# Split weight tiles moved by 64 bytes where they are TensorE's stationary operand

## The chip, the cores and the metric

The kernel runs on one core of one Trainium2 chip. The time is the device time of one execution in microseconds (us). Before the change it is 2506.83 us, the median of 3 runs (2505.83 to 2507.53).

## The reference

Three layers follow each other on one sequence of 256 tokens of width 2048, all in float32: a block of sliding-window attention and a gated feed-forward, a recurrent mLSTM layer, and a band-attention layer with modulated inputs. Cut to its matrix products:

```python
h = rms_norm(x, mixer_norm)
x = x + attention(h @ w_qkv) @ w_o                                    # first block
x = x + (silu(h2 @ w_gate) * (h2 @ w_up)) @ w_down                    # width 5632
y = mlstm(modulated(x) @ a_w_in) @ a_w_out                            # second block, layer 1
x = x + gate_0 * rmsnorm(y, g_post_0)
k, v = modulated(x) @ kv_w;  q, z = modulated(x) @ b_w_in             # second block, layer 2
y = (band_attention(q, k, v) * silu(z)) @ b_w_out
x = x + gate_1 * rmsnorm(y, g_post_1)
```

With it come products of one vector `c` with `ada_w` and `kv_ada_w`, which give the shifts, scales and gates.

## The kernel before

All weights are streamed once from memory in tiles `w` of 128 partitions x 2 k-tiles x 512 columns (512 KB, 4096 bytes in each partition). Float32 accuracy is bought with three fast products in the format fp32r: ScalarE rounds a weight tile to `wh`, VectorE takes the rest `wl = w - wh`, and the activations have been split in the same way into `xh`, `xl` (or `ah`, `al`). TensorE then adds high x high, high x low and low x high (function `products`, line 267).

There are two ways round. In a chunk of mode "tok" the activations are stationary (128 tokens are loaded as weights of the array) and 512 columns of `wh` or `wl` are streamed through it. In a chunk of mode "wst" 128 columns of `wh` or `wl` are loaded, so they are the stationary operand, and the 256 tokens of `xh` or `xl` are streamed. Mode "wst" is used where the result is wanted with features on the partitions: for q and k of the mLSTM layer (8 chunks, one for each head, each followed by three of mode "tok"), for k of the band attention (4 chunks) and for its q and z (8 chunks). Each of these 20 chunks has 16 k-tiles x 4 column blocks x 3 products = 192 matmuls. A trace names a matmul by its output and then the streamed and the stationary operand: `mm<-wh,xh` is mode "tok", `mm<-xh,wh` is mode "wst".

The list `order` has all slots (a weight tile of a chunk) one after the other. `stream_load` (line 138) issues the DMA of a slot from SyncE up to 4 slots ahead, into 3 buffers; `stream_split` (line 146) splits a slot up to 3 ahead, into 4 buffers of `wh` and 4 of `wl`, which are used in turn whatever the mode. Work beside it (softmax, norms, transposes, the vector products) is fed in between by a planner that counts times of its own (`pump`, `stall`); TensorE's part in it has outputs named `bg`.

The memory of a partition is given out in the order of the pools: `keep` first, with `cols`, `onesr`, `mods`, `x`, `xh`, `xl`, `ah`, `al`, `big`; then `strm` with the 3 buffers of `w`, 4 of `wh`, 4 of `wl` and 2 of `mvt`; then `rest`, `small`, and the pool of the phase (`p1` to `p4`). The buffers of one name lie one behind the other at the tile's size. In the last phase this reaches almost to the end of the memory, with `sq` of pool `p4` as its last tile: a scratch tile of 2048 bytes a partition into which `fin_half` (line 1235) has ScalarE write squares that nobody reads (only their sum is kept).

Of the kernel before, what the change touches and what calls it, by code (L numbers as in the profile page):

```python
# [10 lines left out]
F32 = mybir.dt.float32  # L11
F32R = mybir.dt.float32r
# [6 lines left out]
P = 128  # L19
# [2 lines left out]
KD = D // P  # L22
SL = 2
CW = 512
NEG = -1.0e30
EPS = 1e-6
DFF = 5632
# [53 lines left out]
def kernel(ctx: ExitStack, tc: tile.TileContext, i: dict, out: bass.AP):  # L81
# [6 lines left out]
    strm = ctx.enter_context(tc.tile_pool(name="strm", bufs=1))  # L88
    rest = ctx.enter_context(tc.tile_pool(name="rest", bufs=1))
    small = ctx.enter_context(tc.tile_pool(name="small", bufs=4))  # L90
    psp = ctx.enter_context(tc.tile_pool(name="psp", bufs=8, space=PSUM))

    live = [0, 0]
    mmres = [4]
    ver = {"x": [0] * KD, "a": [0] * KD}
# [21 lines left out]
    xh = keep.tile([P, KD, T], F32R, name="xh")  # L117
# [15 lines left out]
    order = []  # L133
# [4 lines left out]
    def stream_load(upto):  # L138
        while cnt["load"] < min(upto, len(order)):
            ch, s = order[cnt["load"]]  # L140
            w = strm.tile([P, SL, CW], F32, tag="w", bufs=3, name="w")
            ch.load(s, w)
# [3 lines left out]
    def stream_split(upto):  # L146
        while cnt["split"] < min(upto, len(order)):
            j = cnt["split"]
            w = loaded.pop(j)
            clk.cur = 0.0  # L150
            wh = strm.tile([P, SL, CW], F32R, tag="wh", bufs=4, name="wh")
            S.copy(wh, w)
            wl = strm.tile([P, SL, CW], F32R, tag="wl", bufs=4, name="wl")
            V.tensor_sub(wl, w, wh.bitcast(F32))
            split[j] = (wh, wl, clk.cur)
            cnt["split"] += 1
# [54 lines left out]
    def wload(w, r0, c0):  # L211
        def f(s, t):
            a = w[r0 + s * SL * P:r0 + (s + 1) * SL * P, c0:c0 + CW]
            nc.sync.dma_start(out=t, in_=a.rearrange("(k p) n -> p k n", p=P))
# [11 lines left out]
    def do_group(idxs):  # L226
        staged = len(idxs) > 1
        ch, s0 = order[idxs[0]]
        for k in range(s0 * SL, (s0 + len(idxs)) * SL):
            while ver[ch.need[0]][k] < ch.need[1][k]:  # L230
                stall()
        stream_load(idxs[0] + 1 + PF)
        stream_split(idxs[0] + 1 + SP)
        if s0 == 0:
            shp = [P, CW] if ch.mode == "tok" else [P, 2, T]
            while live[0] + live[1] > 6:
# [3 lines left out]
        for ts in ((0,), (1,)) if staged else ((0, 1),):  # L240
            for j, idx in enumerate(idxs):
                s = order[idx][1]
                if j and ts[0]:
                    stream_load(idx + 1 + PF)
                    stream_split(idx + SP)
                wh, wl, t_w = split.pop(idx) if ts[-1] else split[idx]
                for k in range(SL):
                    kt = s * SL + k
                    clk.cur = max(t_w, rdy[ch.need[0]][kt])
                    products(ch, kt, k, wh, wl, ts)  # L250
                    ch.k = kt + ts[-1]
                    if not staged:
                        mv_step()
                    if kt < ch.nk - 1:
                        pump()
            if s == ch.ns - 1:
                clk.cur = clk.eng["pe"]
                if ch.part is not None:
                    for t in ts:
                        ch.part(ch.ps, t)  # L260
                if ts[-1]:
                    if not (ch.done and ch.done(ch.ps)):
                        mm_free()
                    ch.ps = None
                pump()
# [52 lines left out]
    def mv_jobs():  # L318
        for lab, w, c0, b, kind, dst in (
                [("A", i["ada0"], j * CW, i["ada_b"][0:1, j * CW:(j + 1) * CW], "col", (0, j // 4, j % 4))  # L320
                 for j in range(8)]
# [134 lines left out]
        return b.rearrange("p a b -> p (a b)")  # L456

    def sumsq(junk_pool, src, dst, scale=1.0):
        j = junk_pool.tile([P, CW], F32, tag="sq", bufs=1, name="sq")
        S.activation(j, src, ACTF.Square, scale=scale, accum_out=dst)  # L460

    def xt_pair(m):
# [83 lines left out]
    ssx = rest.tile([P, 2, 4], F32, name="ssx")  # L546
# [208 lines left out]
    def resid(n, ps, pool, after):  # L755
        for t in range(2):
            c = x[:, t, n * CW:(n + 1) * CW]
            V.tensor_add(c, ps[t], c)
            sumsq(pool, c, ssx[:, t, n:n + 1])
        add_bg(after(n))  # L760
# [36 lines left out]
    pools = {}  # L797
# [50 lines left out]
    def down_part(ps, t):  # L848
        c = x[:, t, 3 * CW:]
        V.tensor_add(c, ps[t], c)  # L850
        sumsq(pools["q2"], c, ssx[:, t, 3:4])
        if t:
            add_bg(xt_raw(3, raw))
# [146 lines left out]
    def num_task(h, v):  # L1000
# [22 lines left out]
        for t in range(2):  # L1023
            sumsq(q3, nm[t], ss[:, t:t + 1], scale=rd[:, t:t + 1])
# [143 lines left out]
    def band_head(g, j):  # L1168
# [5 lines left out]
        nc.sync.dma_start(out=bi, in_=bass.AP(tensor=rel.tensor, offset=h * 383, ap=[[1, P], [1, T]]))  # L1174
        G.memset(bi[0:64, 0:64], NEG)
        yield 1
# [57 lines left out]

    def fin_half(ps, t, n):
        c = pools["yy"][:, t, n * CW:(n + 1) * CW]
        sumsq(pools["q4"], ps[t], ssx[:, t, n:n + 1])
        V.tensor_mul(c, ps[t], gt[1][:, n * CW:(n + 1) * CW])

    def fin_done(n):  # L1240
        def f(ps):
            for t in range(2):
                fin_half(ps, t, n)
        return f

    def fin_part(ps, t):
        fin_half(ps, t, 3)
        x_rstd((t,))
        for n in range(4):
            c = x[:, t, n * CW:(n + 1) * CW]  # L1250
            y = pools["yy"][:, t, n * CW:(n + 1) * CW]
            if n == 3:
                S.activation(y, y, ACTF.Copy, scale=rst[:, t:t + 1])
                G.tensor_add(c, c, y)
            else:
                V.scalar_tensor_tensor(c, y, rst[:, t:t + 1], c, op0=ALU.mult, op1=ALU.add)
        for n in range(4):
            nc.sync.dma_start(out=out[t * P:(t + 1) * P, n * CW:(n + 1) * CW], in_=x[:, t, n * CW:(n + 1) * CW])
# [39 lines left out]
    S.activation(warm, ones[:, 0:1], ACTF.Exp)  # L1298
    stream_load(1)
    stream_split(1)  # L1300
    load_x(0)
    nc.sync.dma_start(out=cols, in_=i["cols"])
# [35 lines left out]
def _lay(inputs):  # L1338
# [10 lines left out]
    r = np.arange(P)  # L1349
    lo = np.where(r[None, :] <= r[:, None], f(0), f(NEG)).astype(f)  # L1350
    up = np.where(r[None, :] > r[:, None], f(0), f(NEG)).astype(f)
    ge = np.where(r[None, :] >= r[:, None], f(0), f(NEG)).astype(f)
    inv = np.power(10000.0, -np.arange(0, 64, 2) / 64.0).astype(f)
# [33 lines left out]
```

## Time and profile before

| | |
|---|---|
| median of 3 runs | 2506.83 us (2505.83 to 2507.53) |
| the profiled execution | 2509.79 us, of which its span 2508.0 us |
| TensorE, matmuls | 97% of the span |
| VectorE, ScalarE, GpSimd | 70%, 48%, 7% |
| mean granted TensorE clock | 0.989 of full |
| read from memory | 571.25 MB, 229 GB/s over the span |

The span runs from the first to the last instruction. Matmuls overlap in the pipeline, so the duration of one is longer than the time between two starts; what a stream of matmuls costs is read from the starts.

### The profile page before, as it was taken

To read this page: it belongs to the slowest core of one execution; us is meant where nothing else is said; L and a number is where in the kernel's file an instruction comes from. 1 tells how busy PE (TensorE), PEld (TensorE's weight loads), DVE (VectorE), ACT (ScalarE), POOL (GpSimd) and SP (SyncE) were. 2 spreads that over 40 slices of the span, in tenths; PEclk is the share of its full clock that TensorE was granted. 3 is DMA by queue.
4 is the path that set the end of the run, shared out by engine and by line. 5 is a ranking of instruction groups with operands and counts; after the bars stand their busy time and mean duration, and the time that the engine had idled before them with its cause. 6 is when DMAs were issued, how large, how long until landed. Compare 5 with 4: busy or idle time off the path is not lost.

```text
span 2508.0 us, 34570 instructions
## 1 busy us (share of the span) xinstructions
PE 2438.4 (97%) x12782; PEld 2076.4 (83%) x12782; DVE 1752.8 (70%) x2577; ACT 1210.1 (48%) x1654; POOL 173.4 (7%) x174
## 2 busy tenths in 40 slices
PE   8989999999999999899999999999999899999998
PEld 6867888887888888778888788888888789899986
DVE  6885777777777777768778777755454664577765
ACT  5665544334443444554445444445444544555553
POOL 0232000000000000201101100101101120000000
PEclk9989999999999999999999999999999999999999
DMA  6524788888888887568878788856556456678854
GB/s 211 157 96 143 238 285 284 286 275 279 287 283 291 285 286 267 159 213 269 264 250 273 267 286 277 261 170 192 182 169 196 151 151 186 193 254 263 259 188 153
DMA packets 319226, 575.63 MB, mean 230 GB/s; under 512 B 21680, under 2 KB 56752, under 8 KB 319056
## 3 DMA queue, kind: packets, MB, share of 16 engines
q1 hardware_dynamic: 319056, 573.42, 70.8%
q8 instruction: 100, 1.64, 0.3%
q14 instruction: 70, 0.57, 0.1%
HBM read 571.25 MB, written 2.10 MB: 229 GB/s over the span
## 4 chain that ended last, share of the span: by engine, by line
PE 77%; DVE 7%; DMA 6%; issue 4%; ACT 4%; POOL 2%; SPq 0%; ACTq 0%; DVEq 0%; POOLq 0%
PE mm L66 72%; PE bg L66 5%; DVE wl L66 3%; ACT wh L66 2%; DMA w<-in_a_w_in_dram 2%; DVE mvacc L66 2%; DMA w<-in_w_gate_dram 1%; DMA w<-in_w_down_dram 1%; POOL big L66 1%; DMA w<-in_w_qkv_dram 1%; ACT big L66 1%; POOL y L66 0%; DMA w<-in_a_w_out_dram 0%; POOL so L66 0%; ACT sq L66 0%
## 5 line engine op out<-in xcount | busy, mean ns | idle before, releaser
L66 DVE TENSOR_TENSOR wl<-w,wh 128x1024 fp32r<-128x1024 f32 x816 | 1009.3, 1244 | 620.9 <-ACT wh L66 605.4
L66 ACT CAST wh<-w 128x1024 fp32r<-128x1024 f32 x816 | 854.9, 1051 | 957.1 <-PE mm L66 598.8
L66 PE MATMUL mm<-wh,xh 128*128 128x512 f32 x1760 | 691.4, 393 | 0.0
L66 PE MATMUL mm<-wh,xl 128*128 128x512 f32 x1760 | 686.8, 390 | 3.8 <-DVE xl L66 3.8
L66 PE MATMUL mm<-wl,xh 128*128 128x512 f32 x1760 | 686.8, 390 | 3.0 <-DVE wl L66 3.0
L66 DVE SCALAR_TENSOR_TENSOR mvacc<-mvt,sc,mvacc 128x512 f32<-128x512 f32 x512 | 392.2, 766 | 10.1 <-issue 0.5
L66 PEld LDWEIGHTS mm<-wh,xl 128*128 128x128 f32 x1760 | 331.1, 188 | 74.3 <-DVE xl L66 4.7
L66 PEld LDWEIGHTS mm<-wl,xh 128*128 128x128 f32 x1760 | 331.2, 188 | 72.2 <-DVE wl L66 5.1
L66 PEld LDWEIGHTS mm<-wh,xh 128*128 128x128 f32 x1760 | 331.2, 188 | 70.5 <-issue 2.6
L66 PE MATMUL mm<-xh,wh 128*128 128x256 f32 x1280 | 370.0, 289 | 7.9 <-DVE xh L66 7.9
L66 PE MATMUL mm<-xl,wh 128*128 128x256 f32 x1280 | 367.5, 287 | 1.0 <-DVE xl L66 0.9
L66 PE MATMUL mm<-xh,wl 128*128 128x256 f32 x1280 | 365.6, 286 | 0.0
L66 PE MATMUL mm<-wh,al 128*128 128x512 f32 x864 | 337.8, 391 | 3.5 <-DVE al L66 3.5
L66 PE MATMUL mm<-wh,ah 128*128 128x512 f32 x864 | 340.3, 394 | 0.0
L66 PE MATMUL mm<-wl,ah 128*128 128x512 f32 x864 | 337.5, 391 | 0.0
L66 PEld LDWEIGHTS mm<-xh,wh 128*128 128x128 f32 x1280 | 249.2, 195 | 11.6 <-DVE xh L66 5.5
L66 PEld LDWEIGHTS mm<-xl,wh 128*128 128x128 f32 x1280 | 249.1, 195 | 4.4 <-DVE xl L66 3.5
L66 PEld LDWEIGHTS mm<-xh,wl 128*128 128x128 f32 x1280 | 249.1, 195 | 0.0
L66 PEld LDWEIGHTS mm<-wh,al 128*128 128x128 f32 x864 | 163.0, 189 | 38.1 <-DVE al L66 3.9
L66 PEld LDWEIGHTS mm<-wh,ah 128*128 128x128 f32 x864 | 162.9, 189 | 36.7 <-issue 3.3
L66 PEld LDWEIGHTS mm<-wl,ah 128*128 128x128 f32 x864 | 163.0, 189 | 33.2 <-DVE wl L66 0.3
L66 POOL TENSOR_TENSOR so<-so,sz 128x512 f32<-128x512 f32 x16 | 29.6, 1851 | 711.8 <-DVE mvacc L66 361.8
(191 smaller groups left out, 1303.2 us busy)
## 6 DMA issues: line engine op xcount, KB each, us to landing
mvt<-in_ada_dram SPq DMA_DIRECT2D x192, 512.0 KB
w<-in_a_w_in_dram SPq DMA_DIRECT2D x192, 512.0 KB
w<-in_w_gate_dram SPq DMA_DIRECT2D x88, 512.0 KB
w<-in_w_up_dram SPq DMA_DIRECT2D x88, 512.0 KB
w<-in_w_down_dram SPq DMA_DIRECT2D x88, 512.0 KB
mvt<-in_kv_ada_dram SPq DMA_DIRECT2D x64, 512.0 KB
w<-in_a_w_in_dram SPq DMA_DIRECT2D x128, 256.0 KB
w<-in_a_w_out_dram SPq DMA_DIRECT2D x64, 512.0 KB
```

The costliest lines, as they stand in the source:

```text
L66: return fn(*a, **k)
```

## The change

`wh` and `wl` are now taken from tiles that are 16 elements (64 bytes) longer. For a slot of mode "wst" the tile's data begin 64 bytes behind the start of the tile, for one of mode "tok" at its start. The eight tiles need 512 bytes more in each partition; in the last phase the scratch tile `sq` is given up for it, and the squares go into the first two k-tiles of `xh`.

```diff
+ROOM = 16
...
+    def offset_tile(tag, off):
+        t = strm.tile([P, SL * CW + ROOM], F32R, tag=tag, bufs=4, name=tag)
+        return t[:, off:off + SL * CW].rearrange("p (k n) -> p k n", n=CW)
...
             w = loaded.pop(j)
+            off = ROOM if order[j][0].mode == "wst" else 0
             clk.cur = 0.0
-            wh = strm.tile([P, SL, CW], F32R, tag="wh", bufs=4, name="wh")
+            wh = offset_tile("wh", off)
             S.copy(wh, w)
-            wl = strm.tile([P, SL, CW], F32R, tag="wl", bufs=4, name="wl")
+            wl = offset_tile("wl", off)
             V.tensor_sub(wl, w, wh.bitcast(F32))
...
     def sumsq(junk_pool, src, dst, scale=1.0):
-        j = junk_pool.tile([P, CW], F32, tag="sq", bufs=1, name="sq")
+        if junk_pool is None:
+            j = xh[:, 0:2].rearrange("p k t -> p (k t)")
+        else:
+            j = junk_pool.tile([P, CW], F32, tag="sq", bufs=1, name="sq")
         S.activation(j, src, ACTF.Square, scale=scale, accum_out=dst)
...
-        sumsq(pools["q4"], ps[t], ssx[:, t, n:n + 1])
+        sumsq(None, ps[t], ssx[:, t, n:n + 1])
```

## Rows read from the trace of the kernel before

**Rows 1.** The page's busy times by engine, its line of granted clock in 40 slices, and the chain of work that ended last, by engine and by line.

```profile
PE 2438.4 (97%) x12782; PEld 2076.4 (83%) x12782; DVE 1752.8 (70%) x2577; ACT 1210.1 (48%) x1654; POOL 173.4 (7%) x174
...
PEclk9989999999999999999999999999999999999999
...
PE 77%; DVE 7%; DMA 6%; issue 4%; ACT 4%; POOL 2%; SPq 0%; ACTq 0%; DVEq 0%; POOLq 0%
PE mm L66 72%; PE bg L66 5%; DVE wl L66 3%; ACT wh L66 2%; DMA w<-in_a_w_in_dram 2%; DVE mvacc L66 2%; DMA w<-in_w_gate_dram 1%; DMA w<-in_w_down_dram 1%; POOL big L66 1%; DMA w<-in_w_qkv_dram 1%; ACT big L66 1%; POOL y L66 0%; DMA w<-in_a_w_out_dram 0%; POOL so L66 0%; ACT sq L66 0%
```

**Rows 2.** The page's costliest groups of instructions: busy us, mean ns of one, then idle time before them. The two splits, and one of the three matmul forms of each kind (the other two forms of a kind have the same count).

```profile
L66 DVE TENSOR_TENSOR wl<-w,wh 128x1024 fp32r<-128x1024 f32 x816 | 1009.3, 1244 | 620.9 <-ACT wh L66 605.4
L66 ACT CAST wh<-w 128x1024 fp32r<-128x1024 f32 x816 | 854.9, 1051 | 957.1 <-PE mm L66 598.8
L66 PE MATMUL mm<-wh,xh 128*128 128x512 f32 x1760 | 691.4, 393 | 0.0
...
L66 PE MATMUL mm<-xh,wh 128*128 128x256 f32 x1280 | 370.0, 289 | 7.9 <-DVE xh L66 7.9
...
L66 PE MATMUL mm<-wh,ah 128*128 128x512 f32 x864 | 340.3, 394 | 0.0
```

**Rows 3.** Timeline of TensorE in the chunks 2 to 4 of the band attention's k (mode "wst"): start us, duration us. The first two and the last two of 576 matmuls.

```profile
2039.92 0.28 PE L66 MATMUL mm<-xh,wh 128*128 128x256 f32 x1
2040.04 0.28 PE L66 MATMUL mm<-xl,wh 128*128 128x256 f32 x1
...
2108.80 0.28 PE L66 MATMUL mm<-xl,wh 128*128 128x256 f32 x1
2108.92 0.28 PE L66 MATMUL mm<-xh,wl 128*128 128x256 f32 x1
```

**Rows 4.** Timeline of TensorE in the feed-forward (mode "tok"). The first and the last of 25 matmuls in a row.

```profile
410.72 0.39 PE L66 MATMUL mm<-wh,xl 128*128 128x512 f32 x1
...
416.16 0.39 PE L66 MATMUL mm<-wh,xl 128*128 128x512 f32 x1
```

**Rows 5.** Timeline of TensorE in the first chunk of the mLSTM layer (mode "wst"), at half clock (see rows 6). The first and the last of 11 matmuls in a row.

```profile
1024.91 0.41 PE L66 MATMUL mm<-xh,wl 128*128 128x256 f32 x1
...
1027.04 0.41 PE L66 MATMUL mm<-xh,wh 128*128 128x256 f32 x1
```

**Rows 6.** Table by stretch: us, busy us of PE, PEld, DVE, ACT and POOL with instructions begun or running, granted clock, busy share of the DMA engines, GB/s. The stretch of rows 5; the first chunk of the band attention's k; its chunks 2 to 4; its eight chunks of q and z.

```profile
1024.50:1027.00 2.50, 2.50 (x13) 2.50 (x13) 1.89 (x3) 2.50 (x4) 2.50 (x4) 0.50 0.00 0
...
2007.00:2040.00 33.00, 29.32 (x193) 26.39 (x194) 27.31 (x42) 18.30 (x27) 13.58 (x15) 0.90 0.37 113
...
2040.00:2109.00 69.00, 69.00 (x577) 69.00 (x576) 29.41 (x24) 28.23 (x30) 0.00 (x0) 1.00 0.64 191
...
2196.00:2409.00 213.00, 212.25 (x1752) 210.49 (x1751) 162.28 (x303) 116.61 (x190) 3.58 (x18) 1.00 0.77 251
```

**Rows 7.** Timeline of TensorE in the gates of the mLSTM layer: fp32r matmuls with 40 stationary columns at a pitch of 160 bytes for each k-tile. The first, two in the midst, and the last of 48, and the matmul after them.

```profile
1060.97 0.28 PE L66 MATMUL bg<-xh,wgh 128*40 128x256 f32 x1
...
1061.55 0.28 PE L66 MATMUL bg<-xh,wgl 128*40 128x256 f32 x1
1061.66 0.28 PE L66 MATMUL bg<-xh,wgh 128*40 128x256 f32 x1
...
1066.46 0.28 PE L66 MATMUL bg<-xh,wgl 128*40 128x256 f32 x1
1066.58 0.40 PE L66 MATMUL mm<-wh,xh 128*128 128x512 f32 x1
```

**Rows 8.** Timeline of TensorE around one of the pairs that sum up a gate vector over the partitions (`mv_reduce`), inside a chunk of mode "wst".

```profile
2344.77 0.28 PE L66 MATMUL mm<-xh,wl 128*128 128x256 f32 x1
2344.89 0.28 PE L66 MATMUL bg<-acch,onesr 128*128 128x256 f32 x1
2345.00 0.28 PE L66 MATMUL bg<-accl,onesr 128*128 128x256 f32 x1
2345.12 0.28 PE L66 MATMUL mm<-xh,wh 128*128 128x256 f32 x1
```

**Rows 9.** Timeline of TensorE behind two interruptions by other matmuls: in mode "wst", 8 matmuls from the second one on (first and last shown), then in mode "tok", 6 matmuls from the second one on (first and last shown).

```profile
2224.11 0.28 PE L66 MATMUL mm<-xl,wh 128*128 128x256 f32 x1
...
2224.93 0.28 PE L66 MATMUL mm<-xh,wl 128*128 128x256 f32 x1
...
417.50 0.39 PE L66 MATMUL mm<-wl,xh 128*128 128x512 f32 x1
...
418.66 0.39 PE L66 MATMUL mm<-wh,xh 128*128 128x512 f32 x1
```

**Rows 10.** The tile `sq`: its instructions in the last stage, duration ns min/median/max, first and last start us; and the last matmul of mode "wst" in the timeline.

```profile
L66 ACT ACTIVATE sq<-mm x8: 597/598/599, 2447.8 to 2497.8; 128x512 f32<-128x512 f32 x8
...
2408.33 0.28 PE L66 MATMUL mm<-xh,wl 128*128 128x256 f32 x1
```

**Rows 11.** Who waited for whom between 2040 and 2409 us: us in total, times, longest us.

```profile
DVE wl L66 <- ACT wh L66: 112.8, 83, 3.7
ACT wh L66 <- PE mm L66: 97.6, 66, 2.1
ACT wh L66 <- DMA w<-in_b_w_in_dram: 26.8, 17, 3.6
```

## The prediction

> **What bounds the kernel now.** I read the page first: TensorE is busy for 97% of the span at full clock but for a few moments, and matmuls are 77% of the chain that ended last [rows 1]. So what counts is the time from one matmul's start to the next, and I went on to the timeline. In mode "wst" 576 matmuls start from 2039.92 to 2108.92 us without a break: 69.00 us over 575 steps is 120.0 ns each [rows 3]. In mode "tok" 24 steps take 5.44 us, 226.7 ns each [rows 4]. The groups give the counts: 3 x 1280 = 3840 matmuls of mode "wst" and 3 x (1760 + 864) = 7872 of mode "tok" [rows 2]. At these steps they are 461 and 1784 us, together 90% of the span.
>
> What would a step be without any loss? A chunk of mode "wst" that begins at half clock shows it: 10 steps take 2.13 us, 213 ns [rows 5], at a granted clock of 0.50, that is 1.2 GHz [rows 6]. This is 256 columns at one per cycle, with nothing on top (256 / 1.2 = 213.3). At full clock, 2.4 GHz, that would be 106.7 ns, so each step of 120.0 ns loses 13.3 ns. In mode "tok" 512 columns would be 213.3 ns, and the step of 226.7 loses the same 13.3 ns. The loss shows only where the streamed operand is read at full speed while the next stationary operand is loaded. That is what the change can aim at: two read streams of TensorE that get in each other's way because of where they begin.
>
> **The change part by part.** Nothing is added to or taken from the instructions: the same 816 splits, the same matmuls, the same DMAs and queues. What moves is addresses.
>
> *Where things lie before.* From `xh` to the first buffer of `wh` there are 5 x 16384 + 3 x 4096 = 94208 bytes, 23 x 4096, and every buffer is 4096 bytes long. The slices used are 512 or 1024 bytes apart. So both operands of every pair begin at the same place within any 512 bytes. The trace of the kernel before shows no other case in a long stream of 128 stationary columns.
>
> *Where they lie after.* A tile is now 4160 bytes long, and the four buffers lie behind each other: buffer n begins 64 x n bytes further within 256 bytes (`wl` likewise, since 4 x 4160 = 65 x 256). In mode "wst" the data then lie 64, 128, 192 and 256 bytes behind the activations' place, in mode "tok" 0, 64, 128 and 192. Within 128 bytes that is: every second slot of *both* modes is off by 64, not all of one and none of the other. The change does only half of what it says in mode "wst", and does in mode "tok" what it says it avoids.
>
> *Price of a shift in mode "wst".* Not in the trace, so from its nearest rows. Upper end of the gain: the whole loss, 13.3 ns. Lower end: none, or a loss, since a new offset can be worse. Between: in the gates, whose 40 stationary columns are at a new offset for each k-tile, 48 steps take 5.61 us, 116.9 ns each, and single steps go down to some 110 (the view rounds to 10 ns) [rows 7]. And the pair `acch`, `accl`, which by the allocation lies 64 bytes off `onesr` within 128, is entered from steps of 120 ns and takes 230 ns from 2344.89 to 2345.12, about 3 to 5 ns less a step [rows 8]. Against it: behind an interruption, where only the timing of the two streams has changed and no address, 7 steps take 0.82 us, 117 ns each [rows 9], before they settle at 120. So 117 needs no offset. Nearest row: a gain of 3 ns, which over half the matmuls is 3 x 1920 = 5.8 us. The first chunk of the band layer is paced by its activations (193 matmuls in 33 us, where 192 x 0.12 = 23 us [rows 6]), and the mLSTM's first one runs at half clock in part [rows 5], so 18 chunks of 20 count: 5.2 us at most from this row, and I take 0 for the forecast, because the same 117 is there without any shift.
>
> *Price of a shift in mode "tok".* Also unseen. Lower end: nothing, or a gain of up to 13.3 ns. On the other side stand the steps behind an interruption: 5 of them take 1.16 us, 232 ns each [rows 9], 5.3 ns more than the settled 226.7. So a change of phase between the two streams costs in this mode. Over half the matmuls, 3936, each ns is 3.9 us. Forecast 0; both ends go into the range.
>
> *The splits.* ScalarE (1051 ns) and VectorE (1244 ns) write the same bytes to other addresses [rows 2]. A slot of mode "wst" is 24 x 120 ns = 2.88 us, so both have more than half of it free in chunks 2 to 4 of k (29 and 28 us busy of 69 [rows 6]). Without that cover a 1% slower split would be 12 ns x 816 = 10 us; the cover is there. In the stretch of q and z VectorE is busy for 162 of 213 us [rows 6], and the split of `wl` waits 113 us in all for `wh`, mostly for buffers and data [rows 11]. A shorter step there would pass on less than whole.
>
> *The squares into `xh`.* Eight instructions of 598 ns, the first at 2447.8, write fp32r instead of f32, no wider. Their new wait, for the last matmul that reads `xh`, is met: it started at 2408.33 [rows 10], 39 us earlier. Nothing is queued behind a wait. Cost 0; without that cover it would be the end of that matmul, once.
>
> The sum: 2506.83 + 0. The profiled execution took 2509.79 us, 1.79 of them outside its span, and lies 0.12% above the median; differences of its rows are used against the median.
>
> A rule that speaks against the change: the Trainium skill, "SBUF — State Buffer", section "Who interferes with whom", gives TensorE two read ports, one for the streamed operand and one for the loads, independent, and says that it never waits on anyone. By that an offset changes nothing, and the sum is the forecast. The trace only half agrees: half clock has no loss, full clock loses 13.3 ns, which two free ports would not explain. The page "TensorE: Matmul & The Clock Gate", section "Wait — 56ns, not 53.3ns?", puts a fixed 2.5 ns on a matmul at full clock; by it the step could fall to 109.2 ns, an estimate of 10.8 x 3840 = 41 us for the whole of mode "wst". No run here shows such a step for 128 stationary columns.
>
> **The rivals.**
>
> *Faster: the offset frees the streams in mode "wst".* For it: the loss of 13.3 ns is there, and steps of fp32r between 110 and 120 ns are seen. Against: 40 stationary columns at many offsets still lose 10 ns. With 7 ns (half the loss) on half of 18 chunks, 1728 matmuls, it is 12 us: 2494.7. At the end of the bounds, 13.3 ns on half of them, 23 us: 2484; a gain of 3 ns in both modes (1728 and 3936 matmuls) would be 17 us: 2490.
>
> *Slower: the rotation of the buffers shifts the streamed tiles.* Every second slot of mode "tok" is off by 64 bytes. If that costs what a change of phase costs [rows 9], 5.3 x 3936 = 21 us are lost, and 3 x 1728 = 5.2 us won in the other mode: 2522.5. It decides from 1.3 ns a step on (5 us / 3936) where mode "wst" gains nothing, from 2.6 where it gains 3. For it: mode "tok" has twice the matmuls, and 232 ns is seen. Against: that row is a change of timing, not of address. If it held for three slots in four, 5904 matmuls, 31 less 8 us: 2530.
>
> *No change, since the change doesn't do what it says.* Either the loss belongs to the load itself and no address matters, or the shifts in both modes cancel. This is the forecast.
>
> **How the numbers follow.** Forecast, no difference: 0.40. Faster: 0.32. Slower: 0.28. About 0.2%, 5 us, is what a measurement of this kernel can tell from no change. The likeliest alone reaches from 2502 to 2511. The other two take the range to 2488 (about 0.1 lies below: most of the loss gone in the even slots) and 2525 (about 0.1 above: the streamed slots lose more than the row says).
>
> **What would show it.** Steps of 120 and 226.7 ns in all four buffers: no address matters, forecast right. Steps in mode "wst" that change from slot to slot (24 matmuls) with the buffer: an offset matters; their period, 2 or 4 slots, tells whether 128 or 256 bytes count. The same in mode "tok" decides the sign. I am wrong if the step of the shifted slots falls to near 107 ns, or if slots of mode "tok" pass 228 ns.

## The result, and the profile after

The changed kernel takes 2524.07 us (2521.41 to 2526.99, 4 runs) where the kernel before takes 2506.33 (2505.11 to 2507.53) beside it: a ratio of 1.0071, 95% interval 1.0054 to 1.0088, so 13.5 to 22 us slower. The time lies inside the range given (2488 to 2525), but the forecast, no difference, was wrong. Its profiled span is 2522.1 us.

First the page: busy times, the line of granted clock, the chain by engine, and three of the costliest groups (busy us, mean ns of one, idle time before).

```profile
PE 2456.7 (97%) x12782; PEld 2066.6 (82%) x12782; DVE 1757.8 (70%) x2577; ACT 1206.3 (48%) x1654; POOL 172.8 (7%) x174
...
PEclk9999999999999999999999999999999999999999
...
PE 78%; DVE 6%; DMA 5%; issue 5%; ACT 4%; POOL 2%; SPq 0%; ACTq 0%; DVEq 0%; POOLq 0%
...
L67 DVE TENSOR_TENSOR wl<-w,wh 128x1024 fp32r<-128x1024 f32 x816 | 1011.5, 1247 | 630.3 <-ACT wh L67 611.4
L67 ACT CAST wh<-w 128x1024 fp32r<-128x1024 f32 x816 | 852.3, 1048 | 972.3 <-PE mm L67 707.1
L67 PE MATMUL mm<-wh,xh 128*128 128x512 f32 x1760 | 697.6, 396 | 0.0
```

Against [rows 1, 2] only TensorE's matmuls have grown: 18.3 us more busy time with the same 12782 instructions at the same clock. The two splits cost what they did (1247 and 1048 ns), and the time that TensorE stands without a matmul has not grown (2522.1 less 2456.7 is 65.4 us, 69.6 before). So the time is again in the steps from one start to the next.

In mode "wst", the timeline of TensorE in chunk 2 of the band attention's k (start us, duration us). The first and the last matmul of each of four slots in a row.

```profile
2056.87 0.28 PE L67 MATMUL mm<-xh,wh 128*128 128x256 f32 x1
...
2059.48 0.28 PE L67 MATMUL mm<-xh,wl 128*128 128x256 f32 x1
2059.59 0.28 PE L67 MATMUL mm<-xh,wh 128*128 128x256 f32 x1
...
2062.35 0.28 PE L67 MATMUL mm<-xh,wl 128*128 128x256 f32 x1
2062.47 0.28 PE L67 MATMUL mm<-xh,wh 128*128 128x256 f32 x1
...
2065.08 0.28 PE L67 MATMUL mm<-xh,wl 128*128 128x256 f32 x1
2065.20 0.28 PE L67 MATMUL mm<-xh,wh 128*128 128x256 f32 x1
...
2067.92 0.28 PE L67 MATMUL mm<-xh,wl 128*128 128x256 f32 x1
```

A slot has 24 matmuls, so 23 steps: 113.5, 120.0, 113.5 and 118.3 ns. All were 120.0 in [rows 3]. In mode "tok" a slot has 12 matmuls, 11 steps; the same view in the feed-forward, for four slots in a row:

```profile
396.57 0.39 PE L67 MATMUL mm<-wh,xh 128*128 128x512 f32 x1
...
399.14 0.39 PE L67 MATMUL mm<-wh,xl 128*128 128x512 f32 x1
399.38 0.39 PE L67 MATMUL mm<-wh,xh 128*128 128x512 f32 x1
...
401.92 0.40 PE L67 MATMUL mm<-wh,xl 128*128 128x512 f32 x1
402.17 0.39 PE L67 MATMUL mm<-wh,xh 128*128 128x512 f32 x1
...
404.69 0.39 PE L67 MATMUL mm<-wh,xl 128*128 128x512 f32 x1
404.92 0.39 PE L67 MATMUL mm<-wh,xh 128*128 128x512 f32 x1
...
407.44 0.39 PE L67 MATMUL mm<-wh,xl 128*128 128x512 f32 x1
```

Steps of 233.6, 230.9, 229.1 and 229.1 ns (to within 1 ns, as the view rounds), where [rows 4] has 226.7. The step changes from slot to slot and comes back after four, so it goes with the place of the buffer. By the allocation the buffers are taken in the order 0, 3, 2, 1, so the four slots above lie 64, 0, 192 and 128 bytes behind the activations' place in mode "wst", and 192, 128, 64 and 0 in mode "tok" (all within 256). A run that sets the four distances of mode "tok" itself bears this order out (tok_rotates, below: means of 228.8, 230.4, 232.9 and 233.0 ns at 0, 64, 128 and 192; here 229.6, 229.2, 231.9 and 233.3). The last slot, at 0, has the old address; its mean is held up by the first steps after the shifted slot, of 229 to 235 ns, before it settles at 227.

From here on "mean step" is that of all steps of a mode in the profile, with breaks left out (over 140 ns in "wst", over 260 in "tok"). Mode "wst" falls from 119.82 to 116.57 ns, mode "tok" rises from 227.04 to 231.09. The sum is 3.25 x 3840 = 12.5 us saved and 4.05 x 7872 = 31.9 lost, +19.4; the median gives +17.7, the spans +14.1.

The table by stretch shows the two signs in one layer: chunks 2 to 4 of k ("wst"), the four of v ("tok"), the eight of q and z ("wst"). Columns as in [rows 6].

```profile
2056.87:2123.94 67.07, 67.07 (x579) 67.07 (x578) 29.43 (x25) 28.41 (x31) 0.00 (x0) 1.00 0.64 196
2123.94:2212.60 88.66, 88.66 (x386) 72.10 (x385) 45.09 (x51) 43.46 (x52) 0.00 (x0) 1.00 0.63 189
2212.60:2420.90 208.30, 206.76 (x1748) 205.22 (x1747) 161.63 (x301) 115.29 (x189) 3.55 (x18) 1.00 0.78 256
```

The same view of the kernel before for v:

```profile
2109.00:2196.10 87.10, 87.10 (x386) 72.14 (x385) 45.05 (x51) 43.70 (x52) 0.00 (x0) 1.00 0.64 191
```

Between the same matmuls (the windows of [rows 6] begin and end a little beside them) k took 69.1 us before and q and z 212.3. So k is 2.0 us shorter, q and z 4.0, and v 1.6 longer. But mode "tok" has twice the matmuls: the first stage alone, from the first matmul to the mLSTM layer, with 4032 of them, went from 1011.8 to 1022.9 us. (1011.8 is long for the old steps: the profiles of sq_only, exact_256, wst_rotates and exact_52 below, which have them too, show 1006.0 to 1009.1.)

### The profile page after: what moved, and what is told of

It reads as the page before. It is cut to its first block, busy times and chain, and to the rows that moved or that the text cites. A ratio compares the mean times of both kernels' runs of the same rounds, so it can differ in the third digit from the quotient of the medians.

```text
span 2522.1 us, 34570 instructions
## 1 busy us (share of the span) xinstructions
PE 2456.7 (97%) x12782; PEld 2066.6 (82%) x12782; DVE 1757.8 (70%) x2577; ACT 1206.3 (48%) x1654; POOL 172.8 (7%) x174
## 4 chain that ended last, share of the span: by engine, by line
PE 78%; DVE 6%; DMA 5%; issue 5%; ACT 4%; POOL 2%; SPq 0%; ACTq 0%; DVEq 0%; POOLq 0%
PE mm L67 73%; PE bg L67 5%; DVE wl L67 3%; DMA w<-in_a_w_in_dram 2%; ACT wh L67 2%; DVE mvacc L67 1%; DMA w<-in_a_w_out_dram 1%; DMA w<-in_b_w_in_dram 1%; POOL so L67 1%; POOL y L67 1%; DMA w<-in_w_qkv_dram 1%; POOL big L67 0%; ACT big L67 0%; ACT sq L67 0%; DVE xl L67 0%
## 5 line engine op out<-in xcount | busy, mean ns | idle before, releaser
L67 DVE TENSOR_TENSOR wl<-w,wh 128x1024 fp32r<-128x1024 f32 x816 | 1011.5, 1247 | 630.3 <-ACT wh L67 611.4
L67 ACT CAST wh<-w 128x1024 fp32r<-128x1024 f32 x816 | 852.3, 1048 | 972.3 <-PE mm L67 707.1
L67 PE MATMUL mm<-wh,xl 128*128 128x512 f32 x1760 | 694.0, 394 | 3.6 <-DVE xl L67 3.6
L67 DVE SCALAR_TENSOR_TENSOR mvacc<-mvt,sc,mvacc 128x512 f32<-128x512 f32 x512 | 393.1, 768 | 11.3 <-DMA mvacc<-in_ada_b_dram 1.2
```

What stands on the lines that cost most here:

```text
L67: return fn(*a, **k)
```

## The experiments

Theory: the distance of the two operands' places within 256 bytes sets the step, by another rule in each mode, and the kernel is slower because three buffers of four now stand off in mode "tok". Rivals: the moved squares, the weights' own place in memory, another effect of the longer tiles. The steps and ratios of all runs (ratio to the kernel before on the same chip, with its 95% interval; none for the two kernels that were executed once):

| run | us | ratio | "wst" ns | "tok" ns |
|---|---|---|---|---|
| before | 2506.33 | | 119.82 | 227.04 |
| the change | 2524.07 | 1.0071 (1.0054 to 1.0088) | 116.57 | 231.09 |
| sq_only | 2504.08 | 0.9991 (0.9982 to 1.0001) | 119.82 | 227.01 |
| both_64 | 2511.96 | 1.0019 (1.0008 to 1.0031) | 114.67 | 229.00 |
| exact_256 | 2496.15 | 0.9955 (0.9940 to 0.9969) | 115.20 | 227.02 |
| scan_16B | 2538.68 | | by offset | by offset |
| tok_rotates | 2531.84 | 1.0106 (1.0091 to 1.0121) | 119.83 | 231.21 |
| wst_rotates | 2501.57 | 0.9982 (0.9972 to 0.9992) | 118.17 | 227.02 |
| scan_4B | 2542.63 | | by offset | by offset |
| activations_moved | 2508.78 | 1.0011 (0.9999 to 1.0022) | 115.10 | 229.34 |
| exact_52 | 2495.63 | 0.9959 (0.9945 to 0.9973) | 115.45 | 227.02 |

**sq_only.** The kernel before with the squares in `xh` and no tile `sq`.

```diff
-        sumsq(pools["q4"], ps[t], ssx[:, t, n:n + 1])
+        sumsq(None, ps[t], ssx[:, t, n:n + 1])
```

> The kernel before with one part of the change alone: the squares of the last stage go into the first two k-tiles of xh and the tile sq of the last pool is gone; no address of wh or wl moves. Address theory (the loss of the change comes from where wh and wl lie): no difference, 2506 us, within 0.2%, and the steps stay at 120 and 226.7 ns. Rival (the squares' new place costs): if it carries the whole loss it is 2524 us, with a wait or a longer Square in the last 100 us.

Both steps stay (119.82, 227.01), and the interval of the ratio just holds 1. In the changed kernel the eight squares, by the view of the tile `xh` (min, median and max ns, first and last start):

```profile
L67 ACT ACTIVATE xh<-mm x8: 597/598/600, 2460.9 to 2511.9; 128x512 fp32r<-128x512 f32 x8
```

They take what they took in [rows 10]. This part of the change costs nothing that can be seen.

**both_64.** The kernel before with a spacer of 64 bytes ahead of the buffers. They keep their 4096 bytes, so that every slot of both modes lies at 64. (The second spacer moves what lies behind by 64 more, so that within 128 bytes it stays in its place.)

```diff
+    strm.tile([P, 16], F32, tag="pad", bufs=1, name="pad")
+    rest.tile([P, 16], F32, tag="pad2", bufs=1, name="pad2")
```

> The kernel before with 64 bytes left free ahead of all buffers of strm, so that every buffer of wh and wl, 4096 bytes apart as before, lies 64 bytes off the activations' place, in both modes (a second gap of 64 bytes behind them leaves the other tiles where they were within 128 bytes). Address theory: the offset itself sets the step, so mode wst goes to the 113.6 ns and mode tok to the 233.3 ns that the buffers at 64 bytes have in the changed kernel: 3840 x -6.4 = -25 and 7872 x 6.6 = +52 us, about 2533 us. Rival (not the offset but the change of offset from slot to slot costs): steps back at 120 and 226.7 ns, 2506 us.

Timeline of TensorE, chunks 2 to 4 of k, the first and the last of 576 matmuls:

```profile
2048.34 0.28 PE L66 MATMUL mm<-xh,wh 128*128 128x256 f32 x1
...
2113.51 0.28 PE L66 MATMUL mm<-xh,wl 128*128 128x256 f32 x1
```

65.17 us over 575 steps is 113.3 ns, without the change from slot to slot: the rotation made it. The mean of mode "tok" is 229.00, not 233.3. That figure of the expectation had been put to 64 bytes by counting the buffers in order; they are taken 0, 3, 2, 1, and it belongs to 192; so the 2533 us expected were too many. With 229.00 the terms are 5.15 x 3840 = 19.8 us saved and 1.96 x 7872 = 15.4 lost. That is -4.4, and the run is 4.8 us slower (2 to 8): the saving does not arrive whole. By the shares that arrive in exact_256 and tok_rotates (0.64 and 0.81, at the end) it would be 12.5 lost and 12.7 saved, about 0; the 2 to 8 us beyond that stay unexplained. By stretch, k is 3.8 us shorter and q and z 3.9, but the eight "wst" chunks of the mLSTM layer only 0.5, where the mean step promises 1536 x 5.15 = 7.9. These chunks scatter by some 4 us between profiles (see exact_256), so one profile doesn't settle it.

**exact_256.** The change with tiles longer by 256 bytes instead of 64. Now the buffers keep their place within 256 bytes, and the change does what its words say: "wst" at 64, "tok" at 0 in every slot.

```diff
-ROOM = 16
+ROOM = 64
+OFF = 16
...
-            off = ROOM if order[j][0].mode == "wst" else 0
+            off = OFF if order[j][0].mode == "wst" else 0
```

> The changed kernel with tiles 256 bytes longer instead of 64 (4352 bytes, 17 x 256), so that all buffers lie alike within 256 bytes: mode wst 64 bytes behind the activations' place in every slot, mode tok on it in every slot. This is what the change's words say. Address theory with a period of 256 bytes or less: wst at 113.6 ns in all slots, tok at 226.7, so 3840 x -6.4 = -25 us, of which about 0.9 arrive: 2484 us, faster than both kernels. If 512 bytes count, the odd buffers differ from the even ones. Rival (the change of offset costs, at each change of mode too): 2500 to 2510 us.

It is the fastest but for exact_52: 2496.15 us, though not the 2484 expected. The timeline of chunks 2 to 4 of k, first and last of 576 matmuls, and the table of that stretch and of two chunks of the mLSTM layer:

```profile
2033.39 0.28 PE L68 MATMUL mm<-xh,wh 128*128 128x256 f32 x1
...
2098.56 0.28 PE L68 MATMUL mm<-xh,wl 128*128 128x256 f32 x1
```

```profile
1609.70:1640.20 30.50, 26.99 (x205) 26.19 (x205) 19.56 (x19) 13.73 (x17) 7.76 (x4) 0.89 0.62 194
1710.70:1733.60 22.90, 22.90 (x201) 22.90 (x200) 12.17 (x10) 10.60 (x13) 7.16 (x4) 1.00 0.61 184
2033.44:2098.70 65.26, 65.26 (x578) 65.26 (x578) 29.51 (x25) 28.42 (x31) 0.00 (x0) 1.00 0.66 202
```

The same two chunks of the mLSTM layer in the kernel before:

```profile
1616.40:1644.80 28.40, 26.51 (x205) 25.82 (x204) 18.66 (x19) 12.94 (x18) 7.80 (x4) 0.94 0.66 205
1715.20:1739.10 23.90, 23.90 (x201) 23.88 (x200) 12.02 (x10) 10.69 (x14) 7.14 (x4) 1.00 0.62 180
```

65.17 / 575 is 113.3 ns again; but other streams of this run stand at 117.8 (see exact_52), so its mean is 115.20. The steps say 4.62 x 3840 = 17.7 us saved; the ratio gives 11.3 (8 to 15). What arrives is seen by stretch, between the same matmuls: the chunks 2 to 4 of k are 3.8 us shorter (69.1 to 65.3), q and z (212.3 to 206.9) 5.4 of about 7. A chunk of the mLSTM layer at full clock passes its gain on, 23.9 to 23.0 us. One with a spell at half clock doesn't: the first pair of rows is 28.40 us at a clock of 0.94 against 30.50 at 0.89, and at half clock a step is 213 ns at 64 bytes as it was at 0 in [rows 5] (here 24 steps from 1623.94 to 1629.06 us, behind a wait). The eight "wst" chunks of this layer together give 1.7 us (211.1 to 209.3) where the mean step promises 1536 x 4.62 = 7.1. But sq_only and tok_rotates, with the old "wst" steps, have 207.4 and 207.1 us there: the spells at half clock scatter by 4 us from profile to profile at unchanged steps, so neither a gain nor a lower clock by the shorter steps is shown in this layer.

**scan_16B and scan_4B.** Tiles longer by 256 bytes as above, and an offset that goes with the chunk: in steps of 16 bytes through all 256, then in steps of 4 bytes around the good places. The diff is that of scan_16B; scan_4B takes the offsets from a list (and its time, 2542.63, lies just above the stretch given for it).

```diff
+    made = {"wst": 0, "tok": 0}
...
+        self.off = 4 * (Chunk.made[mode] % 16)
+        Chunk.made[mode] += 1
...
-            off = ROOM if order[j][0].mode == "wst" else 0
+            off = order[j][0].off
```

> As the last one, but the offset is changed from chunk to chunk in steps of 16 bytes, from 0 to 240, in both modes (counted for each mode by itself). It maps the step against the offset. Address theory with a period of 128 bytes: the steps at 128 to 240 bytes repeat those at 0 to 112; with 256 they don't. In mode wst 64 and 192 bytes at 113.6 ns, 0 at 120; in mode tok 0 at 226.7, 64 at 233.3; the offsets between lie between them or show a better one than any kernel has. Rival (no address matters in a settled stream): one step in each mode at all offsets. Its whole time is not of interest: between 2500 and 2540 us.

> Tiles of 4352 bytes; the offset changes from chunk to chunk in steps of 4 bytes: in mode tok from 32 bytes ahead of the activations' place to 32 behind (counted within 256 bytes) and 128 behind, in mode wst from 40 to 88 bytes behind, and 192. Address theory: 0 in mode tok and 64 in mode wst are lone points or the middle of a valley; if blocks of 16 bytes are what collides, 4 to 12 bytes give the step of 0, and the scan in steps of 16 has seen all there is. Rival (fine alignment matters): some offset off the grid of 16 bytes is below 226.7 or 113.3 ns. Its whole time is not of interest: 2500 to 2540 us.

Mean of the steps in ns by the bytes of offset, within slots behind one of the same offset, breaks left out, for most of the offsets tried. In brackets the lowest and highest mean of a chunk, where they are 2 ns or more apart. Mode "wst" has 20 chunks in each run, so one to four for an offset:

| bytes | "wst" | "tok" | bytes | "wst" | "tok" |
|---|---|---|---|---|---|
| 0 | 119.7 | 227.0 (226.6 to 229.1) | 88 | 113.9 | |
| 4 | | 238.0 | 96 | 118.3 | 233.1 |
| 12 | | 228.9 | 112 | 120.1 | 230.8 (229.4 to 231.7) |
| 16 | 118.5 | 231.7 | 128 | 118.9 | 232.7 |
| 20 | | 238.9 (238.0 to 240.0) | 160 | 119.8 | 234.3 |
| 32 | 118.4 | 233.3 | 192 | 117.5 | 233.5 |
| 48 | 120.5 (119.2 to 121.8) | 233.3 | 224 | 116.8 | 233.3 |
| 52 | 113.7 | | 236 | | 228.7 |
| 64 | 114.3 (113.4 to 116.7) | 229.1 | 244 | | 239.9 (238.6 to 240.6) |
| 76 | 116.4 (114.7 to 118.1) | | 252 | | 227.9 |

Two rows of this table as timelines, 71 steps each: mode "tok" at 20 bytes in scan_4B, then at 64 bytes in scan_16B.

```profile
555.78 0.40 PE L68 MATMUL mm<-wh,xh 128*128 128x512 f32 x1
...
572.82 0.40 PE L68 MATMUL mm<-wh,xl 128*128 128x512 f32 x1
```

```profile
533.21 0.39 PE L67 MATMUL mm<-wh,ah 128*128 128x512 f32 x1
...
549.46 0.39 PE L67 MATMUL mm<-wh,al 128*128 128x512 f32 x1
```

17.04 / 71 = 240.0 ns, and 16.25 / 71 = 228.9. In mode "tok" distances 128 bytes apart don't agree (0 with 128, 64 with 192), while even and odd buffers, which lie 256 bytes apart within 512, do (227.1, 227.3, 226.8 and 226.9 ns in the four buffers of exact_256): 128 bytes are no period, and 256 are one. In mode "wst" 0 and 128 differ too (120.0 and 118.3 ns in the changed kernel's four slots above). In mode "tok" none of the 25 other offsets tried beats the old one, 0, so there was nothing to win there by these. In mode "wst" a few places (52, 64, 88) reach 113.3 in one chunk or more. But the step there isn't fixed by the offset alone: 192 bytes stand at 117.5 here and at 113.5 in the changed kernel. So an offset with a single chunk and a high step may not be a bad one.

**tok_rotates and wst_rotates.** The two halves of the change alone, in tiles of 256 bytes more: the offset goes 0, 64, 128, 192 from slot to slot in one mode, and stays 0 in the other.

```diff
-            off = ROOM if order[j][0].mode == "wst" else 0
+            off = 0 if order[j][0].mode == "wst" else OFF * (j % 4)
```

```diff
-            off = ROOM if order[j][0].mode == "wst" else 0
+            off = OFF * (j % 4 + 1) if order[j][0].mode == "wst" else 0
```

> Tiles of 4352 bytes. Mode wst lies on the activations' place in every slot, as before the change; in mode tok the buffers lie 0, 64, 128 and 192 bytes behind it in turn, as in the changed kernel. Address theory: the whole loss of the change is here. The mean step of mode tok is that of the changed kernel, 231.1 ns against 227.0 before, 4.1 x 7872 = 32 us, of which in the changed kernel two thirds arrived in the first stage (11.1 of 16 us): 2526 to 2538 us. Mode wst stays at 120 ns. Rival (the loss comes from the stationary side, or from both being shifted together): under 2515 us.

> Tiles of 4352 bytes. Mode tok lies on the activations' place in every slot; in mode wst the buffers lie 64, 128, 192 and 256 bytes behind it in turn, as in the changed kernel. Address theory: this is the gain that the changed kernel had and lost again. Mean step of mode wst about 116.6 ns, 3.2 x 3840 = 12 us, of which 5 to 10 arrive: 2497 to 2502 us, slower than the kernel with 64 bytes in every slot (2496 us). Mode tok stays at 227 ns. With the run above it adds up to the change: +18 us. Rival (shifts hurt in both modes): 2507 us or more.

By ratio, tok_rotates is 26.6 us slower (23 to 30) and wst_rotates 4.5 us faster (2 to 7). Together that is +22 (18 to 27, the two half-widths added in squares), beside the change's +17.8 (13.5 to 22). The tables, first of tok_rotates (chunks 2 to 4 of k, then v), then of wst_rotates (the same):

```profile
2057.90:2126.80 68.90, 68.90 (x577) 68.90 (x576) 29.41 (x24) 28.26 (x30) 0.00 (x0) 1.00 0.64 191
2126.80:2215.50 88.70, 88.70 (x386) 72.07 (x385) 45.10 (x52) 43.48 (x52) 0.00 (x0) 1.00 0.64 189
```

```profile
2035.00:2103.30 68.30, 68.30 (x579) 68.30 (x578) 29.53 (x25) 28.48 (x31) 0.00 (x0) 1.00 0.64 193
2103.30:2190.40 87.10, 87.10 (x386) 72.11 (x385) 45.06 (x51) 43.79 (x52) 0.00 (x0) 1.00 0.65 191
```

Each touches its own mode and leaves the other. The loss of the change is that of mode "tok", lessened by a gain in mode "wst", and the loss is shown by itself: tok_rotates has the mean step of the change (231.21 and 231.09). The gain is shown by itself only in part. wst_rotates has 118.17 ns, not the 116.6 expected, and its chunks 2 to 4 of k take 68.3 us where the change has 67.1. It holds the same four distances, but in the reverse order (64, 128, 192, 0 against 64, 0, 192, 128 within 256): behind 0 instead of 128 the slots at 64 have 116.8 ns in the mean (114.3 in the change), and behind 128 instead of 0 those at 192 have 117.6 (113.8). So in this mode what came before counts as well.

**activations_moved.** Is it the weights' own place, or their distance from the activations? Here the weight buffers keep their place within 256 bytes (192 and the 64 of `pad` move them by 256), and `xh` to `al` lie 192 bytes further than before, so that the distance is 64 as in both_64. The squares lie in `xh`, to make room.

```diff
+    strm.tile([P, 16], F32, tag="pad", bufs=1, name="pad")
...
+    keep.tile([P, 48], F32, name="gap")
```

> The kernel before with the squares in xh, and with xh, xl, ah, al moved by 192 bytes while all buffers of wh and wl stay on multiples of 256, 4096 bytes apart: seen from the activations the weights again lie 64 bytes behind (256 - 192), in both modes. Theory that the distance between the two operands sets the step: the same steps as where the weights were moved by 64 in both modes, 114.5 to 115 ns in mode wst and 229 in mode tok, and about the same time, 2509 to 2514 us. Rival (the place of the weight tile by itself matters, as the words of the change could also be read): 120 and 226.7 ns, 2506 us.

The steps are those of both_64: 115.10 and 229.34 (there 114.67 and 229.00), not the 119.8 and 227.0 that weights in this same place have at a distance of 0. The distance counts. But chunks 2 to 4 of k, first and last of 576 matmuls, ran otherwise:

```profile
2043.54 0.28 PE L66 MATMUL mm<-xh,wh 128*128 128x256 f32 x1
...
2111.26 0.28 PE L66 MATMUL mm<-xh,wl 128*128 128x256 f32 x1
```

67.72 / 575 = 117.8 ns, where both_64 and exact_256 have 113.3 at the same distance.

**exact_52.** exact_256 with 52 bytes in mode "wst", the place where scan_4B had the lowest steps without a chunk at 117.8.

```diff
-OFF = 16
+OFF = 13
```

> As the kernel with 64 bytes in every slot of mode wst and 0 in every slot of mode tok (tiles of 4352 bytes), but with 52 bytes instead of 64. In that kernel mode wst stood at 113.3 ns in some chunks and at about 117.7 in others, mean 115.2; in the scan the two chunks at 52 bytes stood at 113.3 throughout. Theory that the offset alone decides, and 52 is the better one: mean 113.7 ns, 1.5 x 3840 = 6 us less, of which 3 to 6 arrive: 2490 to 2493 us. Rival (which of the two steps a chunk falls into hangs on how it was entered, not on the offset): again 115 ns in the mean, 2496 us.

Chunks 2 to 4 of k run at 113.3 ns (2034.19 to 2099.36 us over 575 steps), but the first chunk of q and z doesn't. The first and the last of 193 matmuls there:

```profile
2186.54 0.28 PE L68 MATMUL mm<-xh,wh 128*128 128x256 f32 x1
...
2209.58 0.28 PE L68 MATMUL mm<-xh,wh 128*128 128x256 f32 x1
```

23.04 / 192 = 120.0 ns at an offset that elsewhere gives 113.3. Mean step and time are those of exact_256, so the theory that the offset alone decides fell. A stream of matmuls, until another matmul or a pause comes in between, holds one step: at 64 bytes 113.3 or 117.8, at 52 bytes 113.3 or 120.0 (and once 117.8). None of the 139 streams of more than 30 "wst" matmuls in both_64, exact_256, activations_moved and exact_52 passes from one to the other. Behind an interruption it can be the other, also within a chunk. A chunk of the mLSTM layer in exact_256: the first and the last matmul ahead of an interruption, this one, and the second and the last matmul behind it:

```profile
1710.65 0.28 PE L68 MATMUL mm<-xh,wh 128*128 128x256 f32 x1
...
1719.02 0.28 PE L68 MATMUL mm<-xh,wl 128*128 128x256 f32 x1
1719.14 1.03 PE L68 MATMUL bg<-kc,y 128*128 128x128 f32 x8
...
1720.13 0.28 PE L68 MATMUL mm<-xl,wh 128*128 128x256 f32 x1
...
1733.52 0.28 PE L68 MATMUL mm<-xh,wl 128*128 128x256 f32 x1
```

8.37 us over 71 steps are 117.9 ns, and 13.39 over 118 are 113.5. How the streams come in has a part in it: of those that follow a matmul of mode "tok" without a pause all 8 take the longer step in exact_256 and all 8 in exact_52, where "tok" lies at 0, but only 1 of 8 in both_64 and 2 of 8 in activations_moved, where it lies at 64. What sets the step is open.

## Why the prediction was wrong

**The step that failed: the price of a shift in mode "tok".** It was taken as 0 because [rows 9] showed a change of timing and not of address. The measured price is 4.05 ns a step over all 7872 matmuls, 31.9 us by the steps and 26.6 in tok_rotates. By place it is 2.2 ns at 64 bytes, 4.9 at 128, 6.3 at 192, and 2.6 at 0 behind a shifted slot. The row taken as its bound, 5.3 ns, lies among these; that it was a change of timing was no reason to put the price at 0. Whether both losses have one cause, no run shows.

**The price in mode "wst" was set to 0 too, and isn't.** It is 3.25 ns a step in the mean of all slots: 5.5 and 6.0 at 64 and 192 bytes, 1.4 at 128, nothing at 0. So most of it sits on every second slot, as the prediction counted, at twice the 3 ns of its rows 7 to 9. That is near the middle term of the rival on the faster side, 7 ns on half the slots: 12 us there, 12.5 us here by the steps. By itself only 4.5 us were measured, in wst_rotates, whose mean step fell by 1.65. The full loss of 13.3 ns came back nowhere; the lowest step that a stream holds is 113.3.

**The rotation was right, its period wrong.** That four tiles of 4160 bytes walk through the places, so that the change does in mode "tok" what it says it avoids, was read from the allocation and is what happened. But "within 128 bytes every second slot" is not: 128 is no period (232.7 ns against 227.0 at 0), so in mode "tok" three slots of four are off, not two, and the fourth still pays for the first steps behind a shifted slot.

**The rival on the slower side** was the mechanism that held. That its 2522.5 lies near 2524.07 is luck, for the terms have other sizes: 5.2 won and 21 lost there; 12.5 and 31.9 by the steps of the change, 4.5 and 26.6 in the two runs. Its variant of three slots in four, 2530, had the right count and by the steps the right loss (31 us), with 8 us won. The rival "no change" fell by its own mark: steps differ from buffer to buffer.

**A rule of the Trainium skill** had spoken for no effect: the page "SBUF — State Buffer", section "Who interferes with whom", has TensorE's streamed operand and its loads on independent read ports. The runs disagree: in scan_4B the step of the same kind of matmul is 227.0 ns in the chunks at a distance of 0 and 238.0 to 240.0 in those at 20 bytes. What in the memory the two meet at, no run here shows.

**Right were** the price of the splits (1247 and 1048 ns after), that of the squares (sq_only), and the reading that TensorE's step is the bound: all of the difference sits in it. That a shorter step in the stretch of q and z would pass on less than whole also held (5.4 us of 7 in exact_256). The row read for it was too wide, though: the 113 us that `wl` waits for `wh` in [rows 11] are those of k and v too; in the stretch of q and z alone they are 31.6.

## What to carry to other kernels

Where TensorE is the bound, read its step from start to start in each buffer of a rotating tile, and pad such tiles only by whole multiples of the period in which the step repeats (256 bytes here), or the shift meant for one use rotates into all. A distance that helps an operand which is loaded (113.3 instead of 120.0 ns at 64 bytes) can cost where it is streamed (229.1 instead of 227.0), so price both, each with its own number of matmuls. And a bound read from a row in another situation belongs in the sum with some weight and not at 0: here the mean price (4.05 ns) came out near the row that had been set aside (5.3).

## What the runs showed of the hardware

- Four bytes matter: mode "tok" goes from 227.0 ns at 0 to 238.0 at 4 bytes, back to 228.9 at 12, and to 238.0 to 240.0 at 20.
- At one distance a stream of mode "wst" can hold either of two steps until something interrupts it (113.3 and 117.8 ns at 64 bytes, 113.3 and 120.0 at 52). This is not explained here.
- About 0.64 of the time that shorter "wst" steps promise arrives (11.3 of 17.7 us in exact_256), and about 0.8 of what longer "tok" steps cost (26.6 of 32.8 in tok_rotates), though the intervals of the two ratios let the shares overlap (0.44 to 0.85, and 0.7 to 0.9). Part of the "wst" steps lie in chunks with spells at half clock or paced by other work.
